# Softmax on scaled, negated scores, and the mixers' GpSimd steps on VectorE and ScalarE, in a two-layer hybrid model kernel

## The chip, the cores and the metric

The kernel runs on one core of a Trainium2 chip. The engines are called as in the profile: TensorE (PE for matrix products, PEld for its weight loads), VectorE (DVE), ScalarE (ACT), GpSimd (POOL) and SyncE (SP), whose queue issues most DMAs. The metric is the time of one execution in device microseconds (us).

## The reference

Two layers on one sequence of 512 tokens and 1024 channels, each a mixer and a convolutional feed-forward part, all in float32:

```
for i in range(2):
    h = rmsnorm(x, mix_norms[i])
    x = x + (even_mixer(h, positions, ...) if i == 0 else odd_mixer(h, ...))
    x = x + conv_ffn(rmsnorm(x, ffn_norms[i]), ...)
return rmsnorm(x, final_norm)
```

The even mixer has two kinds of attention. Dilated window attention: 12 heads of width 64 in three groups (windows 128, 512, 2048 at strides 1, 4, 16) with rotary positions, whose three outputs are weighted by a softmax over their log-sums, that is, one softmax over the union of the three groups' keys. Latent attention: 12 causal heads of 64 + 32 query and key channels, queries and keys made from normalized low-rank rows.

```
scores = einsum(q, k) * dh ** -0.5          # 64 ** -0.5; latent heads: 96 ** -0.5
scores = where(valid, scores, -inf)
m = max(scores); p = exp(scores - m); l = sum(p); out = (p / l) @ v
```

The odd mixer has a state-space part (16 heads of 64, chunks of 128 tokens; within a chunk a decayed product, between chunks a running state) and 8 heads of stick-breaking attention (log-sigmoids and their reversed cumulative sums in place of a softmax).

## The kernel before, in words

Tokens are in blocks of 128; a tile is 128 partitions by up to 512 columns, float32. Each product is made from high and low parts: an operand is rounded to a high part (ScalarE's copy), the rest is the low part (VectorE's subtraction, or GpSimd's for the feed-forward weights), and three matrix products (high-high, high-low, low-high) are summed in PSUM. `split` (lines 264, 265), `wchunk` (217 to 221, weights: `wraw`, `whi`, `wlo`) and `norm` (330, 331) do this.

Order. TensorE's instructions in the mixers are tied to the order of the program by class `InOrder`. The other engines' queues are ordered by the framework, which plays the program on a simulated timeline and puts next on an engine what is ready by then; every queue is then worked off in order. Class `Stream` holds the projections that fill TensorE between the steps of the heads; numbers such as `F_M` and `F_D0` say how many steps go where.

Even mixer. `run_qk` projects queries and keys of the dilated heads: ScalarE copies the product to `raw` (729), VectorE multiplies the product by the cosine into `rot` (730), four DMAs of SyncE swap the halves of `raw` into `sw` (733), GpSimd multiplies `sw` by the sine (734) and adds it to `rot` (735). Views `q_order` and `k_order` reorder tokens by stride. `run_mla` projects the latent heads (759 to 774); their query tables `qt` are made at 833 to 835. There are 16 heads in a row: 12 latent ones, and 4 that each hold a dilated head of all three groups. A head's `score(i)` makes scores of one block of queries in PSUM for each of four blocks, and calls `softmax`: VectorE adds the mask and takes the row maximum in one instruction (578), multiplies it by minus the scale (580), ScalarE takes the exponential with that as bias and the scale as factor, and sums the row (581), VectorE inverts the sum (582), GpSimd multiplies the row by it (583). While the next head's scores are made, the head's units transpose its probabilities on TensorE (116, `t<-ident,s`), split them to `pth` and `ptl` (600 and 601, or 951 and 952) and multiply by the values (`o<-pth,v`, `o<-ptl,v`); `head_out` adds the two halves (617, 618).

```
nc.vector.tensor_tensor_reduce(out=t, in0=s[:, :n], in1=mask, scale=1.0, scalar=-3.0e38, op0=ALU.add, op1=ALU.max, accum_out=mx)
nc.vector.tensor_scalar(nmx, mx, -scale, None, op0=ALU.mult)
nc.scalar.activation(t, t, AF.Exp, bias=nmx, scale=scale, accum_out=l)
nc.vector.reciprocal(rl, l)
nc.gpsimd.tensor_scalar(t, t, rl, None, op0=ALU.mult)
```

Odd mixer, state-space part. `prepare(g)` makes for each of two groups and four chunks the tile `xd` (1292, on GpSimd for even chunks, on VectorE for odd ones), its split `xdt` (1296, 1297), the skip term (1300) and the decayed `xd` (1302) with its split `xe`; `xd` has two buffers. `states` carries the running state (1318 decays it, 1320 adds, then split to `ph`); `past` multiplies by it (1332) and adds (1334). `weights` and `apply` make a head's decayed weights (`sg`, `mh`) and products (`o<-xdt,mh`, added at 1366). Stick-breaking heads: `score` makes `ab` and its split `sh`, `sl` (1528 to 1536), `sums` the weights and their split `wh` (1559) and `wl` (1560); `strict` cuts the triangle on GpSimd (1510).

The feed-forward parts (340 to 700 and 1100 to 1450 us) run GpSimd for weights' low parts and one product per tile; they are not in the change.

Of the kernel before, what the change touches and what calls it, by code (L numbers as in the profile page):

```python
# [10 lines left out]
F32 = mybir.dt.float32  # L11
# [3 lines left out]
AF = mybir.ActivationFunctionType  # L15
ALU = mybir.AluOpType
PSUM = bass.MemoryType.PSUM

P = 128
# [5 lines left out]
NEG = -1.0e30  # L25
# [14 lines left out]
K_MLA = 384  # L40
# [15 lines left out]
def const_table():  # L56
    c = np.zeros((P, NCONST), np.float32)
    r = np.arange(P)
    q, k = r[:, None], r[None, :]
    c[:, K_ID : K_ID + P] = np.eye(P)  # L60
    c[:, K_TRI : K_TRI + P] = np.where(q >= k, -1.0, 0.0)
    c[:, K_FOLD : K_FOLD + P] = np.where(q % 32 == k % 32, 1.0, 0.0)
    c[:, K_CAUS : K_CAUS + P] = np.where(q <= k, 0.0, NEG)
    c[:, K_CUM : K_CUM + P] = np.where(q <= k, 1.0, 0.0)
    c[:, K_MLA + 384 : K_MLA + 512] = np.where(k <= q, 0.0, NEG)

    t, j = 4 * (q % 32) + q // 32, q % 32
    for i in range(NB):
        near = k <= 32 * i + j
        parts = [k >= t] if i else []  # L70
        parts += [k <= t, near, near & ((k - j) % 4 == 0)]
        for n, ok in enumerate(parts):
            c[:, K_DSW[i] + n * P : K_DSW[i] + (n + 1) * P] = np.where(ok, 0.0, NEG)
    f1 = np.float32(1.0) / np.float32(10000.0) ** (np.arange(32, dtype=np.float32) * np.float32(2.0 / 64))
    f2 = np.float32(1.0) / np.float32(10000.0) ** (np.arange(16, dtype=np.float32) * np.float32(2.0 / 32))
    c[:, K_F1] = f1[r % 32]
    c[:, K_S1] = np.where(r % 64 < 32, -1.0, 1.0)
    c[:, K_F2] = f2[r % 16]
    c[:, K_S2] = np.where(r % 32 < 16, -1.0, 1.0)
    return c  # L80
# [103 lines left out]
class Builder:  # L184
# [386 lines left out]

    def softmax(self, pool, s, n, tag, bufs, scale, mask):

        nc = self.nc
        st = pool.tile([P, 4], F32, tag="st", name=self.nm("st"), bufs=5)
        mx, nmx, l, rl = (st[:, k : k + 1] for k in range(4))
        t = pool.tile([P, n], F32, tag=tag, name=self.nm(tag), bufs=bufs)
        nc.vector.tensor_tensor_reduce(out=t, in0=s[:, :n], in1=mask, scale=1.0, scalar=-3.0e38,  # L578
                                       op0=ALU.add, op1=ALU.max, accum_out=mx)
        nc.vector.tensor_scalar(nmx, mx, -scale, None, op0=ALU.mult)  # L580
        nc.scalar.activation(t, t, AF.Exp, bias=nmx, scale=scale, accum_out=l)
        nc.vector.reciprocal(rl, l)  # L582
        nc.gpsimd.tensor_scalar(t, t, rl, None, op0=ALU.mult)  # L583
        return t
# [59 lines left out]
    def even_mixer(self, pool):  # L644
# [58 lines left out]
        for t in (cr, sr):  # L703
            nc.gpsimd.tensor_tensor(t, t, r, op=ALU.mult)

# [13 lines left out]
        def run_qk(p, g, s):  # L719
            def run(w):  # L720
                for ps in self.proj_pieces(w, xh, xl):
                    yield
                raw = pool.tile([P, T], F32, tag="fr", name=self.nm("raw"), bufs=2)
                sw = pool.tile([P, T], F32, tag="fr", name=self.nm("sw"), bufs=2)
                t = pool.tile([P, T], F32, name=self.nm("rot"), tag="raw", bufs=8)
                view = k_order if s and g else q_order
                if s and not g:
                    view = lambda t, ordered=True: t
                nc.scalar.activation(raw, ps, AF.Copy)
                nc.vector.tensor_tensor(view(t), view(ps, False), view(cr, False), op=ALU.mult)  # L730
                for b in range(4):
                    o_ = b ^ 1
                    nc.sync.dma_start(sw[b * 32 : b * 32 + 32], raw[o_ * 32 : o_ * 32 + 32])
                nc.gpsimd.tensor_tensor(sw, sw, sr, op=ALU.mult)
                nc.gpsimd.tensor_tensor(view(t), view(t), view(sw, False), op=ALU.add)
                raws[p, g, s] = t

            return f"d{p}{g}{s}", lambda: self.wchunk(a["wqk0"][(p * 3 + g) * 2 + s], D), run
# [87 lines left out]


        qt = []
        for e in range(2):
            t = pool.tile([P, T], F32, tag=f"qt{e}", name=f"qt{e}")  # L830
            rows, pe0, pe1 = ((slice(64, 128), slice(0, 32), slice(32, 64)) if e
                              else (slice(0, 64), slice(64, 96), slice(96, 128)))
            nc.scalar.activation(t[rows], qr[rows], AF.Copy)
            nc.vector.tensor_tensor(t[pe0], c2[pe0], qr[pe0], op=ALU.mult)
            nc.vector.tensor_tensor(t[pe1], s2[pe1], qr[pe1], op=ALU.mult)
            qt.append(t)
# [25 lines left out]
        def mla_head(pr, e):  # L862
# [13 lines left out]
            def score(i):  # L876
                qh, ql = mla[pr][0][e]
                kh, kl = kb[e]
                n = (i + 1) * P
                q = slice(i * P, (i + 1) * P)  # L880

                s = self.psum("s")
                self.mm3(s[:, :n], qh[:, q], ql[:, q], kh[:, :n], kl[:, :n], True, True)
                probs[i] = self.softmax(pool, s, n, f"s{i + 1}", (2, 3, 3, 5)[i], 96 ** -0.5, m_mla[:, 512 - n :])

# [18 lines left out]
        def dsw_head(p, e):  # L904
# [16 lines left out]
            def score(i):  # L921
# [15 lines left out]
                mask = masks[:, K_DSW[i] - K_MLA : K_DSW[i] - K_MLA + n]  # L937
                probs[i] = self.softmax(pool, s, n, *(("s4", 5) if i else ("s3", 3)), 64 ** -0.5, mask)

# [178 lines left out]
    def ssd(self, pool, sub, xh, xl, xs, ZS, zs, others):  # L1118
# [166 lines left out]
        def prepare(g):  # L1285

            xds = []
            for c in range(NB):
                x8 = xs[g][:, c].rearrange("p (h d) -> p h d", h=8)
                tq = lambda k: tok[:, k, c, g * 8 : g * 8 + 8, None].to_broadcast([P, 8, 64])  # L1290
                xd = sub.tile([P, 8, 64], F32, tag="xd", name=self.nm("xd"), bufs=2)
                (nc.vector if c % 2 else nc.gpsimd).tensor_tensor(xd, x8, tq(0), op=ALU.mult)
                for q in range(2):
# [5 lines left out]

                nc.gpsimd.tensor_tensor(x8, x8, dbc[:, g * 8 : g * 8 + 8, None].to_broadcast([P, 8, 64]), op=ALU.mult)  # L1300
                if c < NB - 1:
                    nc.gpsimd.tensor_tensor(xd, xd, tq(3), op=ALU.mult)
                    xde[g, c] = self.split(xd.rearrange("p h d -> p (h d)"), sub, "xe", bufs=6)
# [3 lines left out]
        def states(g, c):  # L1307
# [8 lines left out]
            else:  # L1316
                dec = cdec[:, c, g * 8 : g * 8 + 8, None].to_broadcast([P, 8, 64])
                nc.gpsimd.tensor_tensor(cur.rearrange("p (h d) -> p h d", h=8),
                                        state[g, c - 1][0].rearrange("p (h d) -> p h d", h=8), dec, op=ALU.mult)
# [3 lines left out]
        def past(g, c):  # L1323
# [9 lines left out]
                                    po.rearrange("p (h d) -> p h d", h=8), ec, op=ALU.mult)  # L1333
            nc.gpsimd.tensor_tensor(xs[g][:, c], xs[g][:, c], tt, op=ALU.add)

# [105 lines left out]
    def stick(self, pool, sub, zs, y, qkvs, others):  # L1441
# [55 lines left out]
        def head(h):  # L1497
# [41 lines left out]
            def sums(bi):  # L1539
# [19 lines left out]
                nc.vector.tensor_copy(wh[:, :w], ab[:, :w])  # L1559
                nc.gpsimd.tensor_tensor(wl[:, :w], ab[:, :w], wh[:, :w].bitcast(F32), op=ALU.subtract)  # L1560
                hd.w[bi] = wh, wl
# [136 lines left out]
```

## Time and profile before

| | us |
|---|---|
| median of 3 runs | 1465.1 (1463.52 to 1468.44) |
| profiled execution | 1463.86 |
| its span, first to last instruction | 1462.1 |
| TensorE busy | 1388.7 |
| VectorE busy | 863.6 |
| ScalarE busy | 663.2 |
| GpSimd busy | 597.1 |

The granted TensorE clock was 0.985 over the span. A line of a view of groups reads: line of the kernel, engine, operation, output<-inputs by the program's names, shapes, count | busy us, mean ns of one | idle time of the engine just before them, and what ended it. A line of the view of waits reads: who waited <- for whom, us in total, times, longest. A line of the view by stretches reads: the stretch in us, its length, busy time and count of PE, PEld, DVE, ACT and POOL, then granted clock, DMA share and GB/s. Lines such as 113, 116, 221 and 265 are those of helpers, so the tile's name tells what an instruction is for.

### The profile page before, as it was taken

To read this page: it belongs to the slowest core of one execution; us is meant where nothing else is said; L and a number is where in the kernel's file an instruction comes from. 1 tells how busy PE (TensorE), PEld (TensorE's weight loads), DVE (VectorE), ACT (ScalarE), POOL (GpSimd) and SP (SyncE) were. 2 spreads that over 40 slices of the span, in tenths; PEclk is the share of its full clock that TensorE was granted. 3 is DMA by queue.
4 is the path that set the end of the run, shared out by engine and by line. 5 is a ranking of instruction groups with operands and counts; after the bars stand their busy time and mean duration, and the time that the engine had idled before them with its cause. 6 is when DMAs were issued, how large, how long until landed. Compare 5 with 4: busy or idle time off the path is not lost.

```text
span 1462.1 us, 18180 instructions
## 1 busy us (share of the span) xinstructions
PE 1388.7 (95%) x6796; PEld 1146.8 (78%) x6796; DVE 863.6 (59%) x1362; ACT 663.2 (45%) x1085; POOL 597.1 (41%) x391
## 2 busy tenths in 40 slices
PE   7899899899999999999988898998999999999997
PEld 5777687687888888888877677787888888888886
DVE  7878678746555555122668987678555555552124
ACT  5557457535433333222446465777344333333222
POOL 2454445303655555444102420434215555554441
PEclk9999999999999999999999999999999999999998
DMA  4421212122322322333222111111233233223333
GB/s 166 120 62 55 69 55 69 39 81 73 101 93 95 101 101 85 105 92 95 92 72 73 44 44 58 46 58 40 62 101 101 87 102 101 91 97 94 100 98 98
DMA packets 40264, 121.22 MB, mean 83 GB/s; under 512 B 5232, under 2 KB 8304, under 8 KB 40176
## 3 DMA queue, kind: packets, MB, share of 16 engines
q1 hardware_dynamic: 38160, 117.92, 25.4%
q10 hardware_dynamic: 2016, 2.14, 0.5%
q8 instruction: 54, 0.88, 0.3%
q14 instruction: 34, 0.28, 0.1%
HBM read 114.80 MB, written 2.10 MB: 80 GB/s over the span
## 4 chain that ended last, share of the span: by engine, by line
PE 80%; DVE 12%; ACT 4%; issue 3%; POOL 1%; DMA 1%; DVEq 0%; SPq 0%; ACTq 0%; POOLq 0%
PE proj L113 50%; PE o L113 19%; PE z L113 5%; PE s L113 3%; PE t L116 2%; DVE wlo L221 2%; PE t L113 1%; ACT whi L219 1%; DVE mh L265 1%; DVE sg L1351 0%; DVE cv L1150 0%; DVE xs L1366 0%; DVE xl L331 0%; DVE s L578 0%; DVE rot L730 0%
## 5 line engine op out<-in xcount | busy, mean ns | idle before, releaser
L221 POOL TENSOR_TENSOR wlo<-wraw,whi 128x1024 fp32r<-128x1024 f32 (+1 forms) x135 | 315.2, 2336 | 323.7 <-ACT whi L219 323.7
L219 ACT ACTIVATE whi<-wraw 128x1024 fp32r<-128x1024 f32 (+3 forms) x219 | 222.2, 1015 | 365.0 <-PE proj L113 328.7
L113 PE MATMUL proj<-xh,whi 128*128 128x512 f32 x844 | 343.0, 406 | 8.8 <-ACT xh L330 6.7
L113 PE MATMUL proj<-xh,wlo 128*128 128x512 f32 x844 | 334.1, 396 | 1.4 <-DVE wlo L387 1.1
L113 PE MATMUL proj<-xl,whi 128*128 128x512 f32 x844 | 333.9, 396 | 1.2 <-DVE xl L331 1.2
L113 PE MATMUL proj<-act,whi 128*128 128x512 f32 (+1 forms) x748 | 219.3, 377 | 0.0
L113 PEld LDWEIGHTS proj<-xh,whi 128*128 128x128 f32 x844 | 161.3, 191 | 41.0 <-ACT xh L330 8.7
L113 PEld LDWEIGHTS proj<-xh,wlo 128*128 128x128 f32 x844 | 160.9, 191 | 37.6 <-DVE wlo L387 1.5
L113 PEld LDWEIGHTS proj<-xl,whi 128*128 128x128 f32 x844 | 161.2, 191 | 31.3 <-DVE xl L331 3.1
L113 PEld LDWEIGHTS proj<-act,whi 128*128 128x128 f32 x748 | 137.7, 188 | 25.8
L113 PE MATMUL o<-xh,wlo 128*128 128x512 f32 x368 | 143.4, 390 | 0.0
L113 PE MATMUL o<-xh,whi 128*128 128x512 f32 x368 | 143.3, 389 | 0.0
L113 PE MATMUL o<-xl,whi 128*128 128x512 f32 x368 | 143.2, 389 | 0.0
L113 PE MATMUL proj<-act,wlo 128*128 128x512 f32 (+1 forms) x374 | 140.8, 376 | 0.0
L583 POOL TENSOR_SCALAR s<-s,st 128x512 f32<-128x512 f32 (+1 forms) x64 | 81.2, 1274 | 109.4 <-DVE st L582 82.3
L366 DVE TENSOR_TENSOR x<-x,proj 128x512 f32<-128x512 f32 x31 | 21.2, 684 | 171.0 <-PE proj L113 170.9
L221 DVE TENSOR_TENSOR wlo<-wraw,whi 128x1024 fp32r<-128x1024 f32 (+3 forms) x84 | 100.0, 1190 | 27.3 <-ACT whi L219 26.3
L524 DVE SCALAR_TENSOR_TENSOR cv<-gt,cols,cv 128x511 f32<-128x511 f32 x44 | 94.3, 2148 | 35.9 <-ACT cv L523 35.9
L528 POOL TENSOR_TENSOR sl<-sl,rsr 128x512 f32<-128x512 f32 x44 | 57.8, 1313 | 94.3 <-ACT sl L527 94.3
L527 ACT ACTIVATE sl<-cv 128x512 f32<-128x512 f32 x44 | 27.8, 631 | 127.3 <-DVE cv L525 127.3
L533 DVE TENSOR_TENSOR up<-sl,o 128x512 f32<-128x512 f32 x44 | 30.3, 688 | 91.8 <-POOL sl L528 91.8
L265 DVE TENSOR_TENSOR act<-up,act 128x512 fp32r<-128x512 f32 x44 | 63.3, 1438 | 29.3 <-ACT act L264 29.3
(305 smaller groups left out, 2250.9 us busy)
## 6 DMA issues: line engine op xcount, KB each, us to landing
wraw<-in_g SPq DMA_DIRECT2D x44, 512.0 KB, 3.3
wraw<-in_u SPq DMA_DIRECT2D x44, 512.0 KB, 3.3
wraw<-in_d SPq DMA_DIRECT2D x32, 448.0 KB, 3.3
wraw<-in_wqk SPq DMA_DIRECT2D x20, 512.0 KB, 3.5
wraw<-in_d SPq DMA_DIRECT2D x17, 512.0 KB, 3.5
wraw<-in_wx SPq DMA_DIRECT2D x12, 512.0 KB, 3.4
wraw<-in_wv SPq DMA_DIRECT2D x10, 512.0 KB, 3.6
wraw<-in_wz SPq DMA_DIRECT2D x8, 512.0 KB, 3.3
```

The costliest lines, as they stand in the source:

```text
L113: return self._put(self.b.nc.tensor.matmul(*args, **kw))
L116: return self._put(self.b.nc.tensor.transpose(*args))
L219: nc.scalar.activation(hi[:, :n], raw[:, :n], AF.Copy)
L221: (eng or self.lo).tensor_tensor(lo[:, :n], raw[:, :n], hi[:, :n].bitcast(F32), op=ALU.subtract)
L265: nc.vector.tensor_tensor(lo, src, hi.bitcast(F32), op=ALU.subtract)
L366: self.nc.vector.tensor_tensor(self.x[m], self.x[m], ps, op=ALU.add)
L524: nc.vector.scalar_tensor_tensor(c[:, 1:], gt[:, : T - 1], col_(1), c[:, 1:], op0=ALU.mult, op1=ALU.add)
L527: nc.scalar.activation(s, c, AF.Silu)
L528: nc.gpsimd.tensor_tensor(s, s, r, op=ALU.mult)
L533: nc.vector.tensor_tensor(u, s, pu, op=ALU.mult)
L583: nc.gpsimd.tensor_scalar(t, t, rl, None, op0=ALU.mult)
```

## The change

The scale and a minus sign move into the queries: into the copy of `raw` for q (line 729; the cosine product then reads the copy) and into the tables `qt` (833 to 835). The masks' large value changes its sign. `softmax` takes the row minimum of score plus mask, which is then the bias as it is, with factor -1, and the multiplication of line 580 is gone. The normalization goes from GpSimd to ScalarE (583). From GpSimd to VectorE go the two scalings of cosine and sine (704), the sine product and the sum of the rotation (734, 735), in the state-space part lines 1292, 1300, 1302, 1318 and 1334, and in the stick-breaking heads line 1560. On GpSimd stay, in the mixers, four squares and the masks' conversion at the start, `strict`, and constants.

```
-    c[:, K_MLA + 384 : K_MLA + 512] = np.where(k <= q, 0.0, NEG)
+    c[:, K_MLA + 384 : K_MLA + 512] = np.where(k <= q, 0.0, -NEG)
...
-            c[:, K_DSW[i] + n * P : K_DSW[i] + (n + 1) * P] = np.where(ok, 0.0, NEG)
+            c[:, K_DSW[i] + n * P : K_DSW[i] + (n + 1) * P] = np.where(ok, 0.0, -NEG)
...
-    def softmax(self, pool, s, n, tag, bufs, scale, mask):
+    def softmax(self, pool, s, n, tag, bufs, mask):
...
-        mx, nmx, l, rl = (st[:, k : k + 1] for k in range(4))
+        nmx, l, rl = (st[:, k : k + 1] for k in range(3))
         t = pool.tile([P, n], F32, tag=tag, name=self.nm(tag), bufs=bufs)
-        nc.vector.tensor_tensor_reduce(out=t, in0=s[:, :n], in1=mask, scale=1.0, scalar=-3.0e38,
-                                       op0=ALU.add, op1=ALU.max, accum_out=mx)
-        nc.vector.tensor_scalar(nmx, mx, -scale, None, op0=ALU.mult)
-        nc.scalar.activation(t, t, AF.Exp, bias=nmx, scale=scale, accum_out=l)
+        nc.vector.tensor_tensor_reduce(out=t, in0=s[:, :n], in1=mask, scale=1.0, scalar=3.0e38,
+                                       op0=ALU.add, op1=ALU.min, accum_out=nmx)
+        nc.scalar.activation(t, t, AF.Exp, bias=nmx, scale=-1.0, accum_out=l)
         nc.vector.reciprocal(rl, l)
-        nc.gpsimd.tensor_scalar(t, t, rl, None, op0=ALU.mult)
+        nc.scalar.activation(t, t, AF.Copy, scale=rl)
...
         for t in (cr, sr):
-            nc.gpsimd.tensor_tensor(t, t, r, op=ALU.mult)
+            nc.vector.tensor_tensor(t, t, r, op=ALU.mult)
...
-                nc.scalar.activation(raw, ps, AF.Copy)
-                nc.vector.tensor_tensor(view(t), view(ps, False), view(cr, False), op=ALU.mult)
+                nc.scalar.activation(raw, ps, AF.Copy, scale=1.0 if s else -(64 ** -0.5))
+                nc.vector.tensor_tensor(view(t), view(ps if s else raw, False), view(cr, False), op=ALU.mult)
...
-                nc.gpsimd.tensor_tensor(sw, sw, sr, op=ALU.mult)
-                nc.gpsimd.tensor_tensor(view(t), view(t), view(sw, False), op=ALU.add)
+                nc.vector.tensor_tensor(sw, sw, sr, op=ALU.mult)
+                nc.vector.tensor_tensor(view(t), view(t), view(sw, False), op=ALU.add)
...
-            nc.scalar.activation(t[rows], qr[rows], AF.Copy)
-            nc.vector.tensor_tensor(t[pe0], c2[pe0], qr[pe0], op=ALU.mult)
-            nc.vector.tensor_tensor(t[pe1], s2[pe1], qr[pe1], op=ALU.mult)
+            nc.scalar.activation(t[rows], qr[rows], AF.Copy, scale=-(96 ** -0.5))
+            nc.vector.scalar_tensor_tensor(t[pe0], c2[pe0], -(96 ** -0.5), qr[pe0], op0=ALU.mult, op1=ALU.mult)
+            nc.vector.scalar_tensor_tensor(t[pe1], s2[pe1], -(96 ** -0.5), qr[pe1], op0=ALU.mult, op1=ALU.mult)
...
-                (nc.vector if c % 2 else nc.gpsimd).tensor_tensor(xd, x8, tq(0), op=ALU.mult)
+                nc.vector.tensor_tensor(xd, x8, tq(0), op=ALU.mult)
...
-                nc.gpsimd.tensor_tensor(x8, x8, dbc[:, g * 8 : g * 8 + 8, None].to_broadcast([P, 8, 64]), op=ALU.mult)
+                nc.vector.tensor_tensor(x8, x8, dbc[:, g * 8 : g * 8 + 8, None].to_broadcast([P, 8, 64]), op=ALU.mult)
                 if c < NB - 1:
-                    nc.gpsimd.tensor_tensor(xd, xd, tq(3), op=ALU.mult)
+                    nc.vector.tensor_tensor(xd, xd, tq(3), op=ALU.mult)
...
-                nc.gpsimd.tensor_tensor(cur.rearrange("p (h d) -> p h d", h=8),
+                nc.vector.tensor_tensor(cur.rearrange("p (h d) -> p h d", h=8),
...
-            nc.gpsimd.tensor_tensor(xs[g][:, c], xs[g][:, c], tt, op=ALU.add)
+            nc.vector.tensor_tensor(xs[g][:, c], xs[g][:, c], tt, op=ALU.add)
...
-                nc.gpsimd.tensor_tensor(wl[:, :w], ab[:, :w], wh[:, :w].bitcast(F32), op=ALU.subtract)
+                nc.vector.tensor_tensor(wl[:, :w], ab[:, :w], wh[:, :w].bitcast(F32), op=ALU.subtract)
```

More of the change, by code (lines that the diff above doesn't have):

```diff
@@ L883, in score @@
                 self.mm3(s[:, :n], qh[:, q], ql[:, q], kh[:, :n], kl[:, :n], True, True)
-                probs[i] = self.softmax(pool, s, n, f"s{i + 1}", (2, 3, 3, 5)[i], 96 ** -0.5, m_mla[:, 512 - n :])
+                probs[i] = self.softmax(pool, s, n, f"s{i + 1}", (2, 3, 3, 5)[i], m_mla[:, 512 - n :])
             def units():
@@ L937, in score @@
                 mask = masks[:, K_DSW[i] - K_MLA : K_DSW[i] - K_MLA + n]
-                probs[i] = self.softmax(pool, s, n, *(("s4", 5) if i else ("s3", 3)), 64 ** -0.5, mask)
+                probs[i] = self.softmax(pool, s, n, *(("s4", 5) if i else ("s3", 3)), mask)
             def steps(o, blocks, uses):
```

## The prediction

> **What bounds the kernel now.** I read the page first, then the busy time by stage, then the waits of the even mixer, then groups of instructions with shapes kept apart. From the page, the span and the engines' busy time.
>
> ```profile
> span 1462.1 us, 18180 instructions
> PE 1388.7 (95%) x6796; PEld 1146.8 (78%) x6796; DVE 863.6 (59%) x1362; ACT 663.2 (45%) x1085; POOL 597.1 (41%) x391
> ```
>
> TensorE bounds the kernel, and the change removes none of its work. All that can be won or lost is its idle time, 1462.1 - 1388.7 = 73.4 us, and of that only what lies in the two mixers. Busy time by stage: 60 to 340 us is the even mixer's heads, 790 to 930 the state-space part, 930 to 1042 the stick-breaking heads.
>
> ```profile
> core 0: us, PE busy (x) PEld busy (x) DVE busy (x) ACT busy (x) POOL busy (x), PEclk, DMA share, GB/s
> 60.00:340.00 280.00, 255.09 (x1530) 209.30 (x1530) 204.99 (x483) 158.23 (x324) 115.16 (x86) 0.99 0.21 64
> 790.00:930.00 140.00, 122.78 (x614) 97.61 (x613) 116.71 (x192) 83.96 (x174) 39.06 (x32) 0.96 0.15 49
> 930.00:1042.00 112.00, 104.89 (x533) 88.81 (x531) 84.71 (x139) 76.22 (x133) 48.88 (x66) 0.97 0.15 47
> ```
>
> TensorE stands 24.9, 17.2 and 7.1 us in them, 49 us in all: the purse that this change reaches. VectorE is at 73%, 83% and 76%, so in each stage it is the engine next to TensorE, and it is the engine that receives most of the moved work. The even mixer's waits from 55 to 340 us (waiting engine and line, what released it, us in total, times, longest):
>
> ```profile
> POOL s L583 <- DVE st L582: 82.3, 29, 7.4
> ACT s L581 <- DVE st L580: 45.9, 29, 2.9
> POOL sw L734 <- DMA sw<-raw: 20.8, 5, 5.9
> PEld o L113 <- DVE ptl L601: 6.3, 5, 1.9
> PEld t L116 <- POOL s L583: 4.7, 6, 1.4
> PEld o L113 <- DVE st L580: 0.9, 1, 0.9
> ```
>
> Most of TensorE's own waits end with VectorE. Only 4.7 us end with GpSimd's normalization, 0.9 us with the small multiplication of line 580.
>
> **Even mixer: the softmax.** Groups from 60 to 340 us (count | busy us, mean ns | idle before):
>
> ```profile
> L583 POOL TENSOR_SCALAR s<-s,st 128x512 f32<-128x512 f32 x24 | 38.6, 1607 | 78.3 <-DVE st L582 63.2 <-PE t L116 11.2 <-DVE st L580 3.9
> L581 ACT ACTIVATE s<-s,st 128x512 f32<-128x512 f32 x24 | 17.3, 719 | 26.9 <-DVE st L580 26.6
> L581 ACT ACTIVATE s<-s,st 128x384 f32<-128x384 f32 x16 | 9.8, 610 | 8.7 <-DVE st L580 8.5
> L581 ACT ACTIVATE s<-s,st 128x256 f32<-128x256 f32 x12 | 6.1, 506 | 9.4 <-DVE st L580 9.4
> L581 ACT ACTIVATE s<-s,st 128x128 f32<-128x128 f32 x12 | 4.8, 398 | 2.8 <-DVE st L580 1.3 <-POOL s L583 1.3
> L580 DVE TENSOR_SCALAR st<-st 128x1 f32<-128x1 f32 x64 | 9.3, 148 | 0.8
> ```
>
> The 64 multiplications of line 580 go: VectorE loses 9.3 us, and the exponential no longer stands behind an instruction that VectorE often reaches late (45.9 us of ScalarE idle). The minimum costs what the maximum did, the same form; the sign of the masks is a constant. The 64 normalizations go from GpSimd to ScalarE. The nearest rows are the exponentials, same shapes and also one operand per partition: 17.3 + 9.8 + 6.1 + 4.8 = 38.0 us. ScalarE rises from 158.2 to 196.2 us of 280, 70%. A 512-wide normalization takes 0.72 us in place of 1.61, but it now stands in ScalarE's queue and waits there for the reciprocal; queued behind it are the copies that feed transposed probabilities and weights. For TensorE: the 4.7 and 0.9 us go (-5.6). What ScalarE's fuller queue costs no row shows: bounds are 0 (it is idle 30% still) and 9.5 us (a quarter of the 38.0, TensorE waiting for every fourth). I take +2, near the lower end, because no wait of TensorE for ScalarE is among the large ones above. Behind the normalization the next late thing is VectorE's low half `ptl`.
>
> **Even mixer: the rotation.** Whole-run rows of the two GpSimd steps, and of VectorE's nearest ones up to 340 us; then three that price the contention:
>
> ```profile
> L735 POOL TENSOR_TENSOR rot<-rot,sw 128x512 f32<-128x512 f32 x12 | 19.5, 1625 | 0.5
> L734 POOL TENSOR_TENSOR sw<-sw,sin 128x512 f32<-128x512 f32 x12 | 16.2, 1354 | 27.0 <-DMA sw<-raw 20.8 <-DVE st L580 4.0 <-DVE rst L276 2.1
> L730 DVE TENSOR_TENSOR rot<-proj,cos 128x512 f32<-128x512 f32 x12 | 11.9, 994 | 0.1
> L347 DVE TENSOR_TENSOR sq<-sq,sq 128x512 f32<-128x512 f32 x2 | 1.4, 678 | 0.0
> L872 DVE TENSOR_TENSOR kl<-knp,kh 64x512 fp32r<-64x512 f32 x12 | 10.6, 880 | 0.8 <-ACT kh L871 0.6
> L265 DVE TENSOR_TENSOR qk<-rt,qk 128x512 fp32r<-128x512 f32 x12 | 9.5, 793 | 0.1
> L1112 DVE TENSOR_TENSOR qk<-rot,qk 64x512 fp32r<-64x512 f32 x8 | 5.5, 684 | 0.2
> ```
>
> The 12 products with the sine and the two scalings of cosine and sine are contiguous: 14 x 0.678 = 9.5 us more on VectorE. The 12 additions read through the reordering views of line 730: 12 x 0.994 = 11.9 us. Lines 872 and 265 show what GpSimd takes from VectorE: with two inputs in SBUF they average 0.880 and 0.793 us, against 0.684 of the undisturbed 1112: 12 x 0.196 + 12 x 0.109 = 3.7 us come back. VectorE's balance: -9.3 + 9.5 + 11.9 - 3.7 = +8.4 us, 213.4 of 280. In TensorE's time that is between 0 and 8.4; VectorE still idles 24%, so I take +1. The scaled copies of line 729 and 833 and the fused multiplications of 834 and 835 keep their forms, at no cost. For q, line 730 now waits for the copy of line 729, while the projection's bank is free as soon as that copy is done: no price, since rotations are made well ahead of the heads that use them. The four DMAs for each rotation stay where they are, on SyncE's queue; that VectorE now waits for them is a rival below. Even mixer: -5.6 + 2 + 1 = -2.6 us.
>
> **State-space part.** 790 to 930 us, VectorE's groups; then the stretch from 800 to 808 us, and TensorE's two longest gaps in it:
>
> ```profile
> L265 DVE TENSOR_TENSOR mh<-sg,mh 128x512 fp32r<-128x512 f32 x16 | 13.3, 834 | 0.9 <-ACT mh L264 0.9
> L265 DVE TENSOR_TENSOR ph<-stt,ph 128x512 fp32r<-128x512 f32 x6 | 6.5, 1081 | 0.7 <-ACT ph L264 0.7
> L265 DVE TENSOR_TENSOR xe<-xd,xe 128x512 fp32r<-128x512 f32 x6 | 5.6, 952 | 0.0
> L1297 DVE TENSOR_TENSOR xdt<-xd,xdt 128x256 fp32r<-128x256 f32 x12 | 8.2, 720 | 0.5 <-ACT xdt L1296 0.5
> L1366 DVE TENSOR_TENSOR xs<-o,xs 128x256 f32<-128x256 f32 x32 | 13.3, 417 | 2.1 <-POOL xs L1334 1.2 <-PE o L113 0.5
> L1351 DVE TENSOR_TENSOR sg<-sg,cb 128x512 f32<-128x512 f32 x16 | 12.8, 799 | 2.9 <-ACT sg L1348 2.9
> L1292 DVE TENSOR_TENSOR xd<-xs,tok 128x512 f32<-128x512 f32 x3 | 3.7, 1248 | 0.0
> ```
> ```profile
> 800.00:808.00 8.00, 1.59 (x7) 1.30 (x7) 7.48 (x10) 1.99 (x4) 5.09 (x5) 0.77 0.00 0
> ```
> ```profile
> 803.93 0.44 PE L113 MATMUL o<-xdt,mh 128*128 128x128 f32 x2 [3.88 <-DVE xdt L1297]
> 806.90 0.69 PE L113 MATMUL o<-xdt,mh 128*128 128x128 f32 x2 [2.53 <-DVE xdt L1297]
> ```
>
> Moved are 4 + 8 + 6 (lines 1292, 1300, 1302), 4 (1318) and 6 (1334) operations of 128x512; three of the 28 lie before 790 us. On VectorE at 0.684 us: 25 x 0.684 = 17.1 us. What returns, against 0.684 (0.417 for 256 columns): 16 x 0.150 + 6 x 0.397 + 6 x 0.268 + 12 x 0.303 + 16 x 0.115 + 3 x 0.564 = 13.6 us. A GpSimd operation thus costs VectorE 0.54 us by standing beside it, and 0.68 us when VectorE does it itself: +3.5 us on 116.7, nearly a wash, while every moved step leaves a chain that it lengthened by over 1 us. From 800 to 808 us TensorE does 1.59 us of work in 8, with VectorE full and GpSimd at 5.09: two waits, 3.88 + 2.53 us, for line 1297 behind `xd`, slowed there. The granted clock of 0.77 is part of the bill. I take half of 6.4 us as won, -3; the ends are -6.4 (the gap closes) and +3.5 (all of VectorE's balance shows).
>
> [...]
>
> **Stick-breaking heads.** Whole-run row of the moved step, the rows from 930 to 1042 us, and VectorE's fullest 20 us:
>
> ```profile
> L1560 POOL TENSOR_TENSOR wl<-ab,wh 128x384 fp32r<-128x384 f32 x16 | 18.6, 1162 | 11.3 <-DVE wh L1559 9.9 <-PE proj L113 1.4
> L1531 DVE SCALAR_TENSOR_TENSOR ab<-z,ab 128x384 f32<-128x384 f32 x14 | 7.8, 554 | 2.9 <-ACT ab L1530 2.8
> L1510 POOL TENSOR_SCALAR_AFFINE_SELECT ab<-ab 128x128 f32<-128x128 f32 x29 | 12.8, 440 | 29.3 <-DVE ab L1531 21.5 <-ACT ab L1555 7.8
> ```
> ```profile
> 990.00:1010.00 20.00, 15.73 (x74) 12.73 (x73) 19.23 (x30) 13.22 (x26) 8.86 (x10) 0.91 0.17 53
> ```
> ```profile
> ACT ab L1528 <- POOL wl L1560: 9.7, 8, 2.6
> ```
>
> 16 subtractions at 0.554 and 8 wide ones at 0.684 us put 14.3 us on VectorE. The selects of line 1510 stay on GpSimd, so contention lessens but doesn't end. At 990 to 1010 us VectorE has 0.8 us left in 20; 24 in 112 us are 4 in 20, 2.4 us, of which 1.6 come too much. Against that the step takes half as long, and ScalarE's 9.7 us of waiting for it shrink. I take +1; ends -3 and +5.
>
> **Sum.** -2.6 - 3 + 1 = -4.6 us. The profiled execution took 1463.9 us (span 1462.1 and 1.8 around it; 1.2 under the median of 1465.1): 1463.9 - 4.6 = 1459.3, say 1459. A measurement of this kernel can tell about 0.3%, 4.4 us, from no change.
>
> **Rivals.**
> - Slower: VectorE held by a DMA. Line 734 waits for halves that SyncE's queue swaps; GpSimd sat 20.8 us on them in 5 of 12 and nobody minded. VectorE's queue is in order, and behind line 734 would stand `ptl`, `vt` and the low halves of weights. If half of those 20.8 us return there, 10.4 us: 1470. It decides from about 0.75 us a rotation (12 x 0.75 = 9, the gain and the bound). Against it: VectorE has other work 73% of the time, which can be queued ahead.
> - Slower, stronger: ScalarE in the even mixer late for all heads, at the 9.5 us bound and as much again through `ptl` behind it: about 1476. Against it its 30% of idle time.
> - No change: ScalarE's and VectorE's fuller queues (+9.5 in place of +2 on ScalarE) eat the gain: 1467. For it: two of three engines are then above 70%. Against it: the chain from score to probability loses a link.
> - Stick heads pay. The 24 subtractions have two SBUF inputs and stand beside 48 selects; if each is held for one (0.440 us), VectorE gets 10.6 us more, and half of it shows: 1465. [...]
> - Faster by more: the gap at 800 to 808 us closes wholly (-6.4), ScalarE's extra work hides (0), and the stick heads win (-3): 1463.9 - 5.6 + 1 - 6.4 - 3 = 1450.
> - That the multiplication doesn't vanish: excluded, the minimum's accumulator is the bias itself.
>
> **Chances.** My forecast, 1455 to 1463: 0.36 (0.22 of it past the bound, 0.14 within). Faster by more, 1447 to 1455: 0.20; still faster 0.02. No change 0.10; stick heads 0.07 (0.02 of it slower). DMA hold, 1468 to 1475: 0.19. ScalarE late: 0.06. Faster 0.44, same 0.29, slower 0.27. From 1447 to 1471 leaves out 0.02, 0.06 and half of the DMA hold, 0.17.
>
> **What would show it.** Right: no `<- DVE st L580` and no `<- POOL s`; ScalarE some 196 and VectorE some 213 us in the even mixer's heads; VectorE's `mh`, `ph`, `xe` near 0.68 us, its sum there within 4 us of before; TensorE's gap at `o<-xdt,mh` halved. Wrong: VectorE waiting for `sw<-raw` by over 9 us; TensorE waiting for ScalarE's copies; a longer gap at `xdt` because VectorE takes the new steps first. The order in which the framework queues the moved instructions is in no row, and would make it wrong most easily.

## The result, and the profile after

The changed kernel takes 1454.5 us (median; 1453.8 to 1457.0) against 1465.3 us for the kernel before beside it: a ratio of 0.992, 95% interval 0.9899 to 0.9941. That is 10.8 us less. The prediction had 4.6 us less, 1459; the result lies inside its range (1447 to 1471), but half a microsecond below the 1455 to 1463 that it called its own forecast, in the band of its rival "faster by more". The profiled execution took 1457.0 us. Its page:

```profile
span 1455.3 us, 17916 instructions
...
PE 1387.5 (95%) x6796; PEld 1144.5 (79%) x6796; DVE 873.1 (60%) x1376; ACT 693.8 (48%) x1149; POOL 413.5 (28%) x249
```

GpSimd lost 184 us of work, ScalarE gained 31, VectorE only 9.5, although it took over 78 operations and gave up 64 small ones. Busy time of the same stages as before, from the profile after:

```profile
core 0: us, PE busy (x) PEld busy (x) DVE busy (x) ACT busy (x) POOL busy (x), PEclk, DMA share, GB/s
60.00:340.00 280.00, 255.44 (x1531) 208.28 (x1531) 209.15 (x440) 190.21 (x389) 4.83 (x2) 0.99 0.22 64
790.00:930.00 140.00, 124.39 (x621) 99.96 (x620) 117.62 (x220) 84.73 (x176) 4.23 (x6) 0.95 0.15 50
930.00:1042.00 112.00, 108.01 (x556) 90.63 (x555) 91.81 (x164) 77.20 (x135) 21.99 (x43) 1.00 0.16 49
```

TensorE stands 24.6 us in the even mixer's heads (24.9 before), 15.6 in the state-space stretch (17.2), 4.0 in the stick-breaking stretch (7.1). The third column from the end matters too: the granted clock from 930 to 1042 us went from 0.97 to 1.00. To follow a part on its own, its length is taken from one TensorE instruction to another, so that shifts ahead of it don't count (starts read off the timeline, us):

| part | from, to | before | after | after, profiled again |
|---|---|---|---|---|
| even mixer | start, last `t<-ident,s` | 305.8 | 306.0 | 308.5 |
| state products | first to 65th `o<-xdt,mh` | 52.2 | 48.6 | 49.2 |
| stick heads | first `z<-q,q`, last `o<-wl,vq` | 131.5 | 127.2 | 125.8 |

The even mixer, the largest part of the change, gave nothing that can be told: kernels that leave it as it was read 305.8 to 308.8 us below, so this line alone varies by 3 us. The state products gave 3 to 4 us, the stick-breaking heads 4 to 6.

**Even mixer.** Waits of the profile after from 55 to 340 us, and below them one row of the kernel before that the prediction did not show:

```profile
ACT s L581 <- DVE st L579: 27.6, 23, 2.7
...
ACT s L583 <- DVE st L582: 9.4, 22, 1.6
PEld proj L113 <- DVE vt L760: 9.1, 6, 2.0
...
PEld o L113 <- DVE ptl L601: 6.9, 7, 1.5
...
PEld t L116 <- DVE v L629: 3.7, 4, 1.4
```
```profile
PEld proj L113 <- DVE vt L759: 5.8, 4, 1.9
```

The waits on line 580 and on GpSimd's normalization are gone, as forecast. In their place TensorE waits longer for VectorE: 9.1 us for `vt` (5.8 before), 6.9 for `ptl` (6.3), 3.7 for `v`. Groups of the same kernel from 60 to 340 us:

```profile
L583 ACT ACTIVATE s<-s,st 128x512 f32<-128x512 f32 x24 | 17.2, 717 | 4.5 <-DVE st L582 4.5
...
L736 DVE TENSOR_TENSOR rot<-rot,sw 128x512 f32<-128x512 f32 x11 | 11.1, 1011 | 0.1
...
L874 DVE TENSOR_TENSOR kl<-knp,kh 64x512 fp32r<-64x512 f32 x12 | 8.2, 682 | 0.2
...
L265 DVE TENSOR_TENSOR qk<-rt,qk 128x512 fp32r<-128x512 f32 x12 | 8.1, 680 | 0.1
...
L735 DVE TENSOR_TENSOR sw<-sw,sin 128x512 f32<-128x512 f32 x10 | 6.9, 688 | 2.1 <-issue 1.3 <-DMA sw<-raw 0.8
```

Every single price came out: 717 ns for a normalization (0.72 forecast), 0.69 us for the sine's product, 1.01 for the reordering addition, and `kl` and `qk` back at 0.68. VectorE waited 0.8 us in this stretch for the swapping DMAs.

**State-space part.** VectorE's groups from 790 to 930 us after, and TensorE's two longest gaps:

```profile
L1368 DVE TENSOR_TENSOR xs<-o,xs 128x256 f32<-128x256 f32 x32 | 13.1, 415 | 0.9 <-PE o L113 0.8
...
L265 DVE TENSOR_TENSOR mh<-sg,mh 128x512 fp32r<-128x512 f32 x16 | 10.9, 681 | 0.0
...
L1299 DVE TENSOR_TENSOR xdt<-xd,xdt 128x256 fp32r<-128x256 f32 x12 | 4.6, 413 | 0.0
...
L265 DVE TENSOR_TENSOR xe<-xd,xe 128x512 fp32r<-128x512 f32 x6 | 4.1, 683 | 0.0
L265 DVE TENSOR_TENSOR ph<-stt,ph 128x512 fp32r<-128x512 f32 x6 | 4.1, 683 | 1.3 <-ACT ph L264 1.3
```
```profile
802.19 0.44 PE L113 MATMUL o<-xdt,mh 128*128 128x128 f32 x2 [2.04 <-DVE xdt L1299]
805.87 0.69 PE L113 MATMUL o<-xdt,mh 128*128 128x128 f32 x2 [3.24 <-DVE xdt L1299]
```

With GpSimd nearly silent (4.2 us of work), `mh`, `ph`, `xe` and `xdt` run at 0.68 and 0.41 us (0.83, 1.08, 0.95 and 0.72 before), and VectorE's sum is 117.6 against 116.7 us: the wash of the prediction. The gap at `xdt` shrank from 6.4 to 5.3 us only.

**Stick-breaking heads.** The moved subtraction after (groups, 930 to 1042 us), and ScalarE's wait for it:

```profile
L1562 DVE TENSOR_TENSOR wl<-ab,wh 128x384 fp32r<-128x384 f32 x15 | 8.3, 553 | 0.3
...
L1562 DVE TENSOR_TENSOR wl<-ab,wh 128x512 fp32r<-128x512 f32 x8 | 5.5, 686 | 0.4
```
```profile
ACT ab L1530 <- DVE wl L1562: 6.2, 5, 2.6
```

The clock in that part, in stretches of 3.40 us of the kernel before, two pairs of neighbours:

```profile
957.90:961.30 3.40, 1.10 (x4) 0.37 (x3) 3.37 (x6) 2.69 (x6) 1.90 (x3) 1.00 0.10 11
961.30:964.70 3.40, 3.40 (x14) 3.29 (x15) 2.82 (x5) 0.78 (x2) 1.28 (x3) 0.51 0.41 143
1002.30:1005.70 3.40, 1.53 (x11) 1.44 (x12) 3.40 (x7) 3.05 (x5) 0.27 (x1) 1.00 0.00 0
1005.70:1009.10 3.40, 3.40 (x10) 2.73 (x9) 3.21 (x6) 0.00 (x0) 2.70 (x3) 0.50 0.31 77
```

TensorE works 1.10 and 1.53 us of a stretch; in the next one it is never idle, and the granted clock is 0.51 and 0.50. Products of 512 columns start 0.43 us apart there (from 1006.33 us on) and 0.23 us apart after it (from 1009.81 us on). The trace gives each of the two halved stretches 3.41 us; half of that is lost, so by this estimate each costs 1.7 us more than the stall itself. The stall ahead of the second, from the timeline, is a wait for VectorE:

```profile
1004.17 0.66 PE L116 MATMUL t<-ident,gt 128*128 128x128 f32 x4 [1.96 <-DVE gt L1078]
```

TensorE's idlest such stretch from 930 us on after the change:

```profile
990.90:994.30 3.40, 2.43 (x12) 1.75 (x11) 3.37 (x7) 2.82 (x7) 0.74 (x1) 1.00 0.18 72
```

It works 2.43 us there, and no halved stretch follows. One lies earlier in these heads, though, at 922.6 us of the first profile after; the second profile has none in them. So by the same estimate the clock gave 1.7 of the 4.3 us in the first and 3.4 of the 5.7 in the second, and 2.3 to 2.6 us are something else. VectorE is not freed in these heads: over their whole length the subtractions put 14.3 us on it, and the operations that both kernels have there lose 6.5 us. What got shorter are waits: ScalarE's for `wl` (9.7 us before, 6.2 after) and VectorE's for the cut of the triangle, which on GpSimd no longer queues behind subtractions (16.9 before, 12.0 after).

### The profile page after: what moved, and what is told of

Same layout as the page of the kernel before. It is cut to its first block, busy times and chain, and to the rows that moved or that the text cites. A ratio compares the mean times of both kernels' runs of the same rounds, so it can differ in the third digit from the quotient of the medians.

```text
span 1455.3 us, 17916 instructions
## 1 busy us (share of the span) xinstructions
PE 1387.5 (95%) x6796; PEld 1144.5 (79%) x6796; DVE 873.1 (60%) x1376; ACT 693.8 (48%) x1149; POOL 413.5 (28%) x249
## 4 chain that ended last, share of the span: by engine, by line
PE 77%; DVE 13%; ACT 5%; issue 3%; DMA 1%; POOL 0%; SPq 0%; DVEq 0%; ACTq 0%; POOLq 0%
PE proj L113 49%; PE o L113 19%; PE z L113 5%; PE s L113 2%; DVE wlo L221 2%; PE t L116 2%; PE t L113 1%; ACT whi L219 1%; ACT s L581 1%; ACT s L583 1%; DVE xl L331 0%; DVE ptl L601 0%; DVE cv L1152 0%; DVE mh L265 0%; DVE x L366 0%
## 5 line engine op out<-in xcount | busy, mean ns | idle before, releaser
L221 DVE TENSOR_TENSOR wlo<-wraw,whi 128x1024 fp32r<-128x1024 f32 (+3 forms) x84 | 95.6, 1139 | 28.2 <-ACT whi L219 27.4
L265 DVE TENSOR_TENSOR act<-up,act 128x512 fp32r<-128x512 f32 x44 | 63.3, 1438 | 29.3 <-ACT act L264 29.3
L113 PEld LDWEIGHTS proj<-act,wlo 128*128 128x128 f32 x374 | 70.4, 188 | 13.0
```

Source lines behind the costliest of these rows:

```text
L113: return self._put(self.b.nc.tensor.matmul(*args, **kw))
L221: (eng or self.lo).tensor_tensor(lo[:, :n], raw[:, :n], hi[:, :n].bitcast(F32), op=ALU.subtract)
L265: nc.vector.tensor_tensor(lo, src, hi.bitcast(F32), op=ALU.subtract)
```

## The experiments

The theory after the result: (a) the even mixer nets to nothing because its edits cancel; (b) the other two parts win because VectorE's operations no longer stand beside GpSimd's. The rivals: (a') softmax or rotation alone gives a gain that the other edits hide; (b') the parts win because the moved step itself is shorter, wherever GpSimd is.

**Each part alone on the kernel before.** First the softmax: scaled and negated scores, line 580 gone, normalization on ScalarE.

```diff
...
-        nc.vector.tensor_scalar(nmx, mx, -scale, None, op0=ALU.mult)
-        nc.scalar.activation(t, t, AF.Exp, bias=nmx, scale=scale, accum_out=l)
...
+        nc.scalar.activation(t, t, AF.Exp, bias=nmx, scale=-1.0, accum_out=l)
...
-        nc.gpsimd.tensor_scalar(t, t, rl, None, op0=ALU.mult)
+        nc.scalar.activation(t, t, AF.Copy, scale=rl)
...
```

> Only the softmax part on the kernel before: scaled, negated scores, minimum as bias, normalization on ScalarE; rotation, state-space and stick steps stay on GpSimd. Theory 1 (each stage is paid by its own moved steps): the even mixer's heads shorten by 1 to 4 us, everything behind them keeps its length: 1461 to 1464 against 1465. Rival (ScalarE's 38 us more in its queue eat the shorter chain): 0, within 2 us of before, and TensorE's waits for VectorE's ptl and vt grow by about what the waits on the normalization lose (some 5 us). ScalarE some 32 to 38 us busier from 60 to 340 us under both.

Measured: 1464.0 us, ratio 0.9992 (0.9981 to 1.0002). No change that can be told. The rival was nearer: TensorE's weight loads wait no more for the normalization, but 14.9 us in all for `ptl` and `vt` (12.1 before) and 3.8 for `v`.

The rotation and the scaling of cosine and sine:

```diff
...
-                nc.gpsimd.tensor_tensor(sw, sw, sr, op=ALU.mult)
-                nc.gpsimd.tensor_tensor(view(t), view(t), view(sw, False), op=ALU.add)
+                nc.vector.tensor_tensor(sw, sw, sr, op=ALU.mult)
+                nc.vector.tensor_tensor(view(t), view(t), view(sw, False), op=ALU.add)
```

> Only the rotation's product and sum and the scalings of cosine and sine go to VectorE; the softmax stays as before. Theory 1: VectorE gets 21 us in the even mixer and 4 back: TensorE's heads 0 to 4 us longer, 1465 to 1469. Rival (VectorE held by the swapped halves' DMA): VectorE waits over 9 us for sw<-raw in total, 1470 or more.

Measured: 1476.0 us, ratio 1.007 (1.0057 to 1.0084): 10 us slower, which neither theory 1 nor, by its mechanism, the rival foresaw, since VectorE waited only 3.3 us for the swapping DMAs. The even mixer takes 314.9 us, 6 to 9 more than where it is as before. Its waits from 55 to 340 us, TensorE's weight loads:

```profile
PEld t L116 <- POOL s L583: 9.1, 10, 2.4
PEld proj L113 <- DVE vt L759: 8.7, 5, 2.9
```

TensorE waits longer for the softmax chain's last step on GpSimd (9.1 us against 4.7), and the projections stall on `vt` (8.7 against 5.8). Four halved stretches lie in this even mixer against two before (granted clock 0.98 against 0.99 from 60 to 340 us), so up to 3.4 us are clock.

The five operations of the state-space part (lines 1292, 1300, 1302, 1318, 1334 to VectorE):

> Only the state-space part's 28 operations go to VectorE. Theory 1 (GpSimd beside VectorE costs VectorE nearly as much as the operation itself): VectorE's sum from 790 to 930 us within 4 us of before, mh, ph, xe at 0.68 us each, and the part 2 to 4 us shorter: 1461 to 1463. Rival (VectorE is the bound there and simply gets 17 us more): part 3 us or more longer, 1468.

Measured: 1463.5 us, ratio 0.9983 (0.9969 to 0.9997). The state products take 48.6 us. The stick heads, whose code is as before, take 133.9 (131.5 before): four halved stretches fall in them instead of two (granted clock 0.66 from 960 to 970 us), by the estimate above up to 3.4 us.

The subtraction of the stick-breaking heads (line 1560 to VectorE):

> Only the low half wl of the stick-breaking heads goes to VectorE. The changed kernel's trace has these heads 4.3 us shorter, where I had said 1 us longer. If that is this one step's doing: 1460 to 1462 against 1465, with TensorE's idle time in these heads some 4 us less. Rival (the heads start under other conditions because the state-space part changed before them, and the order in which the framework queues them differs): under 1.5 us of gain, and it appears only where p3_states' edit is made too.

Measured: 1459.1 us, ratio 0.9966 (0.9954 to 0.9979), a little more gain than expected. The stick heads take 125.8 us, without a halved clock in them; the state products stay at 51.7.

**The two winning parts together**, without anything of the even mixer:

> The kernel before, with only the five operations of the state-space part and the subtraction of the stick-breaking heads moved to VectorE; softmax, rotation and scaling of the queries as before. If the whole gain lies in these two parts and the even mixer gives nothing net, it should come out where the changed kernel does, 1454 to 1457 us (ratio 0.992 to 0.995): the two parts alone gave -2 and -6 us. If the softmax and the rotation together also bring something, as the prediction had it (-2.6 us), it stays behind the changed kernel, at 1458 to 1461 us.

Measured: 1455.1 us, ratio 0.9923 (0.99 to 0.9947). It is level with the whole change, at 0.992 and, measured again below, 0.9931. State products 49.2, stick heads 125.8 us. Within the intervals, some 3 us, the gain lies in six lines. The two alone add up to 7.5 us by their ratios, together they give 11.3; the intervals don't tell these apart, but the halved stretches of the state-space kernel's stick heads, gone here, would be a reason.

**Pieces of the even mixer taken back from the changed kernel.** The changed kernel once more, beside them:

> The changed kernel unaltered, as the reference for the three beside it: 1453 to 1457. Its trace also tells how much a stage varies from one execution to the next: up to 68 us (the start) by 2 us or more, the state-space and stick parts by under 0.5 us unless TensorE's granted clock differs there.

Measured: 1454.9 us, ratio 0.9931 (0.9915 to 0.9948).

The rotation and the two scalings back on GpSimd, the reverse of the second diff above:

> The changed kernel with the rotation's product and sum and the scalings of cosine and sine back on GpSimd. Alone they cost 10 us on the kernel before. Theory 1 (parts add): without them the changed kernel gains as much, 1443 to 1449. Rival, theory 2 (the cost was that GpSimd's slow normalization and the small multiplication of line 580 stood in the same chains; with both gone VectorE has room, while GpSimd's 24 operations again disturb it): 1453 to 1459, no gain.

Measured: 1456.0 us, ratio 0.9933 (0.9916 to 0.9949).

The normalization back on GpSimd:

```diff
-        nc.scalar.activation(t, t, AF.Copy, scale=rl)
+        nc.gpsimd.tensor_scalar(t, t, rl, None, op0=ALU.mult)
```

> The changed kernel with the normalization back on GpSimd (minimum as bias kept, rotation on VectorE). Theory 2: the rotation on VectorE is bearable only with the normalization on ScalarE: even mixer 4 to 9 us longer, TensorE again waits 4 us or more for the normalization: 1458 to 1463. Rival (ScalarE's 38 us more are a burden): 1450 to 1454.

Measured: 1455.0 us, ratio 0.9937 (0.9913 to 0.996), between the two expectations: theory 2 falls as far as it rested on the normalization. Within some 3 us neither place matters once line 580 is gone, while with line 580 in place the rotation cost 10 us. Rival (a') falls: softmax gives -1 alone (not told from 0), rotation +10 alone, both together about 0. The edits don't add: with the 64 multiplications gone, the rotation costs nothing that can be seen. Whether that is the 9.3 us of VectorE's time, the shorter chain to the exponential, or another order of the queues, which the framework makes anew for each kernel, no run tells apart.

**Contention by itself.** To the changed kernel 25 GpSimd products of 128x512, which nobody reads, are added beside the state-space part:

```diff
...
+        nc.gpsimd.tensor_tensor(gh[:, 0:64], cd, cd, op=ALU.mult)
+        for k in range(25):
+            nc.gpsimd.tensor_tensor(gh, self.x[k % 8], self.x[(k + 1) % 8], op=ALU.mult)
```

> The changed kernel with 25 products of 128x512 on GpSimd beside the state-space part, from the table of decays on, which nobody reads or waits for (two inputs in SBUF, output to a scratch tile). Theory 1 (standing beside VectorE is what GpSimd's work cost): mh, ph and xe of VectorE rise from 0.68 to 0.8 us or more while they run, VectorE's sum from 790 to 930 us by 8 us or more, and the part by 2 to 8 us: 1457 to 1463. Rival (the gain of the part came from shorter chains and another order): VectorE's means may rise, the time doesn't: 1453 to 1456.

Measured: 1480.8 us, ratio 1.0106 (1.0087 to 1.0124): 26 us more than the changed kernel, 1 us for each product, and far more than either expectation had. Groups from 790 to 930 us of this kernel, then TensorE's wait and the stretch as a whole:

```profile
L1289 POOL TENSOR_TENSOR gh<-x,x 128x512 bf16<-128x512 f32 x25 | 40.1, 1603 | 2.0
...
L1374 DVE TENSOR_TENSOR xs<-o,xs 128x256 f32<-128x256 f32 x32 | 13.1, 416 | 1.0 <-PE o L113 0.8
...
L1300 DVE TENSOR_TENSOR xd<-xs,tok 128x512 f32<-128x512 f32 x6 | 8.3, 1381 | 0.0
...
L265 DVE TENSOR_TENSOR xe<-xd,xe 128x512 fp32r<-128x512 f32 x6 | 7.3, 1219 | 0.0
```
```profile
PEld o L113 <- DVE xdt L1305: 18.0, 2, 10.7
```
```profile
790.00:930.00 140.00, 108.14 (x532) 86.63 (x530) 126.58 (x197) 68.44 (x148) 40.73 (x26) 0.89 0.13 42
```

`xd` and `xe`, with two operands in SBUF, take 1.38 and 1.22 us in place of 0.68; line 1374 reads one from PSUM and keeps 416 ns (415 without the ghosts). VectorE's sum rises by 9.0 us, as theory 1 had it, but the state products take 69.6 us (48.6 to 49.2): `xdt`, for which TensorE waits, stands behind the lengthened steps, and the granted clock falls from 0.95 to 0.89, which is 8 of the 140 us. Beside the ghosts the chain that TensorE waits for thus took 20 to 21 us more, the clock's share included. That isn't the price of the 28 operations that the change removed: these ghosts run back to back from 799 to 838 us, where the kernel before had GpSimd busy 39 of 140 us.

The same for the stick-breaking heads: the subtraction on VectorE, and one of the same size on GpSimd into a tensor that is dead by then.

```diff
...
                 nc.vector.tensor_tensor(wl[:, :w], ab[:, :w], wh[:, :w].bitcast(F32), op=ALU.subtract)
+                nc.gpsimd.tensor_tensor(self.gh[:, bi, :w], self.x[7][:, :w], wh[:, :w].bitcast(F32), op=ALU.subtract)
```

> The changed kernel, with the subtraction done on VectorE and once more on GpSimd, at its old place and size, into a tensor that nobody reads any more; no work waits for it except the slot of wh. If the stick-breaking heads won because VectorE no longer stands beside that GpSimd operation, the gain of that part goes back, with the halved clock in it: +3 to +6 us, 1457 to 1461. If they won because the chain from wh through wl to the next copy of ab became shorter, the ghost costs nothing: 1454 to 1456, no halved clock from 930 to 1042 us, and the stage stays at 126 us.

Measured: 1467.4 us, ratio 1.0009 (0.9995 to 1.0024). The whole gain of the change is gone, more than was expected. Its groups from 930 to 1042 us, and two waits there:

```profile
L1564 POOL TENSOR_TENSOR xs<-x,wh 128x384 f32<-128x384 f32 x13 | 17.7, 1362 | 8.8 <-DVE wh L1562 8.8
...
L1563 DVE TENSOR_TENSOR wl<-ab,wh 128x512 fp32r<-128x512 f32 x7 | 10.3, 1475 | 0.3
...
L1563 DVE TENSOR_TENSOR wl<-ab,wh 128x384 fp32r<-128x384 f32 x13 | 10.2, 784 | 0.1
```
```profile
ACT ab L1531 <- DVE wl L1563: 15.1, 14, 2.6
...
PEld o L113 <- DVE wl L1563: 7.7, 6, 2.5
```

The heads take 137.0 us, 10 to 11 more than in the changed kernel. The clock isn't the reason: there is one halved stretch in them, at 926.1 us, as in the first profile of the changed kernel, and from 930 to 1042 us the granted clock is 1.00 in both. So rival (b') falls as it was put: the 24 subtractions are still shorter in sum than they were on GpSimd (24.8 us against 29.3), and the heads are slower. But the ghost starts on the same `wh` at the same time as the subtraction, and of the 14.4 us that VectorE's operations take longer over the whole of these heads, 10.5 are the subtraction itself; ScalarE waits 15.1 us for it (6.2 in the changed kernel), TensorE 7.7 (3.3). In this run GpSimd's work beside it cost more than the change gained there (10 to 11 us against 4 to 6). Whether the change gained by a shorter step (0.55 us in place of 1.16) or by VectorE's other operations (6.5 us back) stays open. The ghosts also put work into GpSimd's queue ahead of the triangle's cut and hold a buffer of `wh`. VectorE's waits for the cut were 8.5 us in all (12.0 in the changed kernel), so that isn't where the time went; ScalarE waited 2.8 us for a ghost.

**The gap that stayed.** If the 5.3 us at `xdt` are what is left, six more pieces of the next projection ahead of the first state products should fill them:

```diff
-        st.fill(F_S)
+        st.fill(F_S + 6)
```

> The changed kernel, with six more pieces of the next projection issued ahead of the first products of the state-space part. If TensorE's gap from 800 to 806 us (5.3 us, and a halved clock of 6.83 us that costs half of its length) is what remains there, the pieces fill it while VectorE gets xd and xdt ready: -3 to -8 us, 1447 to 1452, and no halved clock at 803. If the pieces are missing as cover later in the part, the gap moves and the time stays: 1453 to 1457.

Measured: 1461.4 us, ratio 0.9968 (0.9955 to 0.9982): slower than the changed kernel by 5 to 7 us. The gap fell to one wait of 3.12 us; what the pieces had covered came out later. TensorE's waits of this kernel from 840 to 930 us:

```profile
PE t L113 <- DVE rsy L278: 6.4, 2, 3.4
...
PEld o L113 <- ACT mh L264: 3.9, 2, 3.7
```

From 905 us on the clock is halved for 10.2 us there (granted 0.91 from 840 to 930 us, 0.96 in the changed kernel). The rival expectation (the gap moves) was nearer, and it too was 4 us short.

The same, and the skip terms (line 1302 after) multiplied behind all of `xd`:

> The same, and the multiplication of the skip terms, which VectorE now does between the steps that TensorE waits for, comes after all of them. If VectorE's order within the gap costs time, this gives a further 1 to 3 us. If the pieces cover the gap already, or TensorE waits for the skip terms later, it is level with the kernel that only issues the pieces earlier, within 1 us.

Measured: 1460.6 us, ratio 0.9957 (0.9942 to 0.9972). The intervals of the two overlap; whether VectorE's order matters there stays open. No version beat the changed kernel.

## Why the prediction was right, point by point

The sum was -2.6 - 3 + 1 = -4.6 us; the parts' lengths give about 0, -3.1 to -3.7 and -4.3 to -5.7. The direction and the range held, the distribution over the parts didn't: one part of three came out as forecast, and the measured 10.8 us are more than twice the sum. That the time still fell into the range is partly luck, since what the even mixer didn't give the stick-breaking heads gave, for reasons that the prediction had not counted.

- Even mixer, waits that go, -5.6: the rows vanished, the time didn't. The step that failed is the one that turned TensorE's waits for a released instruction straight into time. VectorE was late next, with `vt` and `v` and not only with `ptl`, and TensorE's idle time there is 24.6 us after 24.9.
- ScalarE's queue, +2: the normalizations cost nothing that can be seen (0.9931 with them, 0.9937 without, within some 3 us). The lower bound was the right one. ScalarE reads 190.2 us there, not 196: the normalizations last 37.7 us in sum, as forecast, but the busy time counts overlapping instructions once.
- Rotation, +1: right in the changed kernel as far as the intervals tell (0.9933 without it, 0.9931 with it), and wrong as a price of its own: alone it is +10, beyond the 8.4 us that stood as its upper bound. The prediction set the 9.3 us of line 580 against the rotation in one balance, and that held: removal and addition could only be priced together.
- VectorE's balance there, +8.4: the windows show 204.99 to 209.15, +4.2. Each row that it was made of measured as forecast, but more came back than the 3.7 us of the two rows that it counted: up to 340 us the operations that both kernels have take 8.9 us less, 3.0 of them the weights' low parts.
- State-space part, -3: measured -3.1 to -3.7, and 0.9983 alone (-2.5 us). The price of contention (0.54 us against 0.68) and the wash held. Where the time came from was half right: of the stage's gain the gap at `xdt` gave 1.1 us; 1.7 us are a halved stretch at 841.9 us of the kernel before. The softmax, rotation and stick-head kernels, which keep that part as it was, have it too (841.1, 850.3 and 844.2 us); the changed kernel and the one with this part alone don't.
- Stick-breaking heads, +1 with ends of -3 and +5: the step that failed, by 5 to 7 us and outside its own ends. It charged VectorE 14.3 us and let nothing return, though it had just priced what a GpSimd operation takes from VectorE (24 x 0.54 = 13.0 us). The rows show +7.1 (84.71 to 91.81 us), so about half returned. And it turned VectorE's fuller time into TensorE's: VectorE had 7 us more to do and the heads were shorter all the same, with TensorE idle 4.0 us in place of 7.1. It also left out the clock: 0.97 in the quoted row of 930 to 1042 us is 0.03 x 112 = 3.4 us, and the row of 990 to 1010 us said 0.91. Of the gain 1.7 to 3.4 us are clock; what made the rest is not separated.
- Rivals. VectorE held by the DMA: 0.8 us in place of 10.4. ScalarE late: no wait of TensorE for it above 2 us. Stick heads pay, if each subtraction is held for a select: that was an estimate, and the profile after shows no such hold (0.553 and 0.686 us a subtraction, where 0.554 and 0.684 were priced); the heads gained 4 to 6 us. Faster by more, 1450: the result lies in its band, and its sum was as near as the forecast's, by other terms: its gap didn't close, and its stick heads gained 3 where 4 to 6 were measured.

About 1 to 3 us of the 10.8 stay unassigned: the parts sum to 7.4 to 9.4. Profiles of one kernel differ by as much, in part through halved stretches that fall in one execution and not in the next (10.24 us of them at 741.7 us in the first profile after, 6.83 at 743.6 in the second).

## What to carry to other kernels

Price a step moved off GpSimd twice: what the receiving engine does more, and what its other operations get back; here the second was nearly as large as the first in the state-space part, and less than half of it in the other two. Where TensorE is fed just in time, read the granted clock of short stretches behind its stalls, for here a stall of 1.96 us was followed by 3.41 us at a granted clock of 0.50, an estimated 1.7 us more. Edits that free and use the same engine had no prices of their own here (the rotation +10 us alone, about 0 beside the softmax), so test them together.

## What the hardware showed that was not expected

Up to 1010 us of both profiles, before and first after, the halved clock came in stretches of 3.41 us, or two or three of them on end (6.83 and 10.24 us), on a fixed grid: in the profile before they start at 804.3, 841.9, 961.3 and 1005.7 us, which lie 11, 35 and 13 times 3.413 us apart. The stretches ahead of the two in the stick-breaking heads had TensorE working for 0.33 and 0.45 of the time. Between 56 and 1010 us of that execution all six stretches at full clock in which it worked for less than 0.5 were followed by a halved one, and of some 20 with 0.55 to 0.75 one was. The share alone didn't decide: in the first profile after, the stretches ahead of 891.9 and 922.6 us had 0.58 and 0.65 and were followed by halved ones, and two with 0.53 weren't. One halved stretch, at 350.3 us, came after a stretch that was 0.93 busy by the records, and why isn't known. The one long idle gap ahead of the halved stretch at 1005.7 us, from 1002.2 us on, lasted 1.96 us.
